# Down projection of a transformer block's SwiGLU in seven block products, weight sums kept in DRAM

## Chip, cores and metric

The kernel runs on one core of one Trainium2 chip. The metric is the device time of one execution in microseconds, median of several runs.

## What is computed

One encoder block for 512 tokens of width 1024: an RMS norm, one combined projection, two kinds of attention, gates, an output projection, and then the channel mixer (width 2816), which is the part that changes:

```python
        h = rms_norm(x, norm_ffn[l])
        x = x + (jax.nn.silu(h @ w_gate_ffn[l]) * (h @ w_up_ffn[l])) @ w_down_ffn[l]

    return rms_norm(x, norm_final)
```

## The kernel before

All data are float32. Each operand of a large matmul is split into a high part in float32r (a cast on ACT, line 68) and the rest (a subtraction on DVE, line 75), and each product is three matmuls, high by high, high by low, low by high (`mm3`, lines 87 to 90). Weights come in units of 128 x 1024 by `load_unit` (lines 77 to 85): SP issues the load into one of 3 raw buffers, ACT casts it to `whi`, DVE subtracts to `wlo`; `whi` and `wlo` have 5 buffers each.

The channel mixer starts at line 585. The 2816 columns are 22 tiles f of 128. `ffn_in(f)` (line 596) computes gate and up of one f for all 512 tokens with 48 matmuls of 128x512 into the PSUM tiles `pg` and `pu` (two buffers each), then ACT takes the sigmoid, DVE multiplies twice into `sg`, and the result is split into `ah` and `al`, which hold the activations of all 22 tiles. The first two f run in two halves of 256 tokens. The down projection multiplies 128-token slices of `ah` and `al` with units of w_down; a unit has two f and one half (512) of the 1024 output columns. For the first column half (units 0 to 10) `down0(u)` runs among the gate/up blocks, 24 matmuls for each pair of f, into four PSUM accumulators `pd`, one for each row tile of 128 tokens. For the second column half (units 11 to 21) the same runs behind the last gate/up block (lines 664 to 674); there the accumulator of the last row tile is in two halves of 256 columns, and the last two units are taken row tile by row tile, so that each row tile can be finished while the next is computed. `residual` (line 649) adds an accumulator to `x1` on DVE, ACT sums the squares, DVE multiplies by the final norm's gain; then POOL takes the power -0.5 (line 683), ACT and DVE scale one half each, and ACT and SP issue the stores of `out`.

The program is written in the order of the work, and a scheduler of the framework places the instructions of each engine by its own estimates; each engine then runs its instructions in that order.

Of the kernel before, what the change touches and what calls it, by code (L numbers as in the profile page):

```python
# [26 lines left out]
NF = FF // P  # L27
UNIT = 1024
# [6 lines left out]
def kernel(  # L35
# [220 lines left out]
    def group_a():  # L256
# [199 lines left out]
    pr = ps_hd.tile([P, S], F32, tag="hd", name="pr")  # L456
# [31 lines left out]
    for qd in range(4):  # L488
# [29 lines left out]
    x1 = x1p.tile([P, NT, DM], F32, name="x1")  # L518
# [42 lines left out]
    accs = [ps_o.tile([P, S], F32, tag="po", name=f"po0_{tt}") for tt in range(NT)]  # L561
# [10 lines left out]
    for tt in range(NT):  # L572
        acc = ps_o.tile([P, S], F32, tag="po", name=f"po1_{tt}")
# [8 lines left out]
    mixer.close()  # L582


    ffn = ExitStack()
    ap_ = pool(ffn, "ap")
    ah = ap_.tile([P, NF, S], F32R, name="ah")
    al = ap_.tile([P, NF, S], F32R, name="al")
# [22 lines left out]
    def down(acc, u, wu, tt, c0=0, c1=S):  # L611
        hi, lo = wu
        t = slice(tt * P, (tt + 1) * P)
        for j in range(2):
            f = 2 * u + j
            w = slice(j * S + c0, j * S + c1)
            mm3(acc, ah[:, f, t], al[:, f, t], hi[:, w], lo[:, w], f == 0, f == NF - 1)
# [15 lines left out]
    for f in range(1, NF):  # L633
        if f > 1:
            ffn_in(f, 0, S, *gu(f))
        if f == 1:
            acc0 = [ps_d.tile([P, S], F32, tag="pd", name=f"pd0_{tt}") for tt in range(NT)]
        if f >= 3 and f % 2 == 1:
            u = (f - 3) // 2
            down0(u)  # L640
    down0(10)
# [14 lines left out]
    v.memset(s3, 0.0)  # L656
    for tt in range(NT):
        residual(tt, 0, S, acc0[tt], 0)
    acc1 = [[(ps_d.tile([P, S], F32, tag="pd", name=f"pd1_{tt}"), 0, S)] for tt in range(NT - 1)]
    H = S // 2  # L660
    acc1.append([(ps_d.tile([P, S], F32, tag="pd", name="pd1_3")[:, :H], 0, H),
                 (ps_g.tile([P, S], F32, tag="pg", name="pd1_4")[:, :H], H, S)])
    NLAST = 2
    for u in range(11 - NLAST):
        wu = load_unit(w_down[11 + u], f"d1_{u}")
        for tt in range(NT):
            for acc, c0, c1 in acc1[tt]:
                down(acc, u, wu, tt, c0, c1)
    last = [load_unit(w_down[11 + u], f"d1_{u}") for u in range(11 - NLAST, 11)]
    for tt in range(NT):  # L670
        for i, (acc, c0, c1) in enumerate(acc1[tt]):
            for u in range(NLAST):
                down(acc, 11 - NLAST + u, last[u], tt, c0, c1)
            residual(tt, S + c0, S + c1, acc, 1 + i)
        n = 1 + len(acc1[tt])
# [93 lines left out]
```

## Time and profile before

| | |
|---|---|
| runs | 767.14, 767.30, 767.84 us; median 767.3 |
| profiled execution | 766.71 us |
| span of its instructions | 764.7 us, 9837 instructions |
| mean granted TensorE clock | 0.995 |
| PE, PE weight load | 745.6 us (97%), 638.5 us (83%) |
| DVE, ACT, POOL | 412.5 us, 337.2 us, 102.7 us |
| DMA | 69.52 MB, 90 GB/s over the span |

The profiled execution lasts 2.0 us longer than the span from its first to its last instruction. Matmuls are pipelined: each lasts longer than the distance to the next, so the busy time of PE says that it had no gap, and the distance of starts says what a matmul costs. A wait is put down to what came last before it.

### The profile page before, as it was taken

The numbers are of one execution on the slowest core, as the hardware profiler recorded it, in microseconds if no ns is written. First come the engines' busy times: TensorE is split into PE (matmuls) and PEld (weight loads), VectorE is DVE, ScalarE is ACT, GpSimd is POOL, SyncE is SP. The second block draws the span as 40 slices with busy tenths as digits, with TensorE's granted clock in tenths as the row PEclk, the third lists the DMA queues.
The fourth block names the chain that finished last, engine by engine and source line by source line (L and its number), as shares of the span: only waits on it lengthen the run. The fifth ranks groups of instructions, "written<-read, shape, count | busy, mean of one in ns | idle before, by whom it ended". The sixth has DMA issues, their size and how long they took to land.

```text
span 764.7 us, 9837 instructions
## 1 busy us (share of the span) xinstructions
PE 745.6 (97%) x3786; PEld 638.5 (83%) x3786; DVE 412.5 (54%) x668; ACT 337.2 (44%) x606; POOL 102.7 (13%) x126
## 2 busy tenths in 40 slices
PE   5999999999999999999999999999999999999996
PEld 4889887799988888888889888888888888888885
DVE  5778698669795564494375433332423333335114
ACT  6457698777667665232153222222222322233203
POOL 3656342223221010100000000000000000000001
PEclk9999999999999999999999999999999999999998
DMA  8122021002141212344223332323232333232202
GB/s 331 64 84 83 29 68 58 21 22 85 29 136 60 78 56 83 137 138 138 82 83 111 111 109 84 110 86 108 86 107 91 102 94 100 90 103 84 82 1 111
DMA packets 21071, 69.52 MB, mean 91 GB/s; under 512 B 2592, under 2 KB 2848, under 8 KB 21024
## 3 DMA queue, kind: packets, MB, share of 16 engines
q1 hardware_dynamic: 18432, 63.45, 25.1%
q10 hardware_dynamic: 2592, 5.45, 2.0%
q8 instruction: 30, 0.49, 0.3%
q14 instruction: 17, 0.14, 0.1%
HBM read 66.79 MB, written 2.10 MB: 90 GB/s over the span
## 4 chain that ended last, share of the span: by engine, by line
PE 94%; DVE 2%; DMA 2%; ACT 1%; issue 1%; POOL 0%; POOLq 0%; ACTq 0%; SPq 0%; DVEq 0%
PE pg L89 5%; PE pu L89 5%; PE pu L90 5%; PE pg L90 5%; PE pg L88 5%; PE pu L88 5%; PE pd L89 5%; PE pd L88 5%; PE pd L90 5%; PE gt L89 4%; PE gt L88 4%; PE gt L90 4%; PE acc_b L89 3%; PE acc_b L88 3%; PE acc_b L90 3%; PE pp L88 2%
## 5 line engine op out<-in xcount | busy, mean ns | idle before, releaser
L89 PE MATMUL pd<-wlo_d,ah 128*128 128x512 f32 (+1 forms) x198 | 72.5, 366 | 0.0
L88 PE MATMUL pd<-whi_d,ah 128*128 128x512 f32 (+1 forms) x198 | 72.4, 366 | 0.0
L90 PE MATMUL pd<-whi_d,al 128*128 128x512 f32 (+1 forms) x198 | 72.0, 365 | 0.0
L88 PE MATMUL pg<-hh,whi_fg 128*128 128x512 f32 (+1 forms) x192 | 71.4, 372 | 0.0
L90 PE MATMUL pu<-hh,wlo_fu 128*128 128x512 f32 (+1 forms) x192 | 71.4, 372 | 0.0
L89 PE MATMUL pg<-hl,whi_fg 128*128 128x512 f32 (+1 forms) x192 | 71.3, 371 | 0.0
L88 PE MATMUL pu<-hh,whi_fu 128*128 128x512 f32 (+1 forms) x192 | 71.3, 371 | 0.0
L89 PE MATMUL pu<-hl,whi_fu 128*128 128x512 f32 (+1 forms) x192 | 71.3, 371 | 0.0
L90 PE MATMUL pg<-hh,wlo_fg 128*128 128x512 f32 (+1 forms) x192 | 71.3, 371 | 0.0
L75 DVE TENSOR_TENSOR wlo_d<-raw_d,whi_d 128x1024 fp32r<-128x1024 f32 x22 | 26.9, 1225 | 72.4 <-ACT whi_d L68 72.4
L75 DVE TENSOR_TENSOR wlo_fg<-raw_fg,whi_fg 128x1024 fp32r<-128x1024 f32 x22 | 27.0, 1225 | 70.0 <-ACT whi_fg L68 69.9
L68 ACT CAST whi_d<-raw_d 128x1024 fp32r<-128x1024 f32 x22 | 23.2, 1053 | 85.4 <-issue 42.3
L68 ACT CAST whi_fg<-raw_fg 128x1024 fp32r<-128x1024 f32 x22 | 23.2, 1053 | 78.8 <-PE pg L89 41.2
L68 ACT CAST whi_fu<-raw_fu 128x1024 fp32r<-128x1024 f32 x22 | 23.2, 1053 | 72.7 <-PE pu L89 69.1
L88 PE MATMUL gt<-xgh,whi_g 128*128 128x512 f32 x128 | 50.6, 395 | 0.0
L90 PE MATMUL gt<-xgh,wlo_g 128*128 128x512 f32 x128 | 50.5, 395 | 0.0
L89 PE MATMUL gt<-xgl,whi_g 128*128 128x512 f32 x128 | 50.5, 394 | 0.0
L683 POOL TENSOR_TENSOR r<-mf,mhalf 128x1 f32<-128x1 f32 x4 | 2.3, 586 | 356.9 <-DVE mf L681 356.9
L607 DVE TENSOR_TENSOR sg<-pu,sg 128x512 f32<-128x512 f32 (+1 forms) x24 | 15.4, 646 | 54.8 <-PE pu L90 54.8
L89 PE MATMUL acc_b<-wlo_b,xgh 128*128 128x384 f32 x128 | 43.6, 341 | 0.0
L90 PE MATMUL acc_b<-whi_b,xgl 128*128 128x384 f32 x128 | 43.4, 339 | 0.0
L88 PE MATMUL acc_b<-whi_b,xgh 128*128 128x384 f32 x128 | 43.3, 339 | 0.0
(278 smaller groups left out, 1832.9 us busy)
## 6 DMA issues: line engine op xcount, KB each, us to landing
raw_fg<-in_w_gu_dram SPq DMA_DIRECT2D x22, 512.0 KB, 3.3
raw_fu<-in_w_gu_dram SPq DMA_DIRECT2D x22, 512.0 KB, 3.3
raw_d<-in_w_down_dram SPq DMA_DIRECT2D x22, 512.0 KB, 3.3
raw_g<-in_w_in_dram SPq DMA_DIRECT2D x16, 512.0 KB, 3.3
raw_b<-in_w_in_dram SPq DMA_DIRECT2D x16, 384.0 KB, 3.6
raw_p<-in_w_proj_dram SPq DMA_DIRECT2D x8, 512.0 KB, 3.3
raw_o<-in_w_out_dram SPq DMA_DIRECT2D x8, 512.0 KB, 3.3
raq<-in_w_in_dram SPq DMA_DIRECT2D x4, 512.0 KB, 7.3
```

Source lines behind the costliest of these rows:

```text
L68: a.copy(dst, src)
L75: v.tensor_tensor(out=dst, in0=src, in1=hi.bitcast(F32), op=ALU.subtract)
L88: pe.matmul(acc, lhsT=lh, rhs=rh, start=start, stop=False)
L89: pe.matmul(acc, lhsT=lh, rhs=rl, start=False, stop=False)
L90: pe.matmul(acc, lhsT=ll, rhs=rh, start=False, stop=stop)
L607: v.tensor_tensor(out=t_, in0=pu, in1=t_, op=ALU.mult)
L683: g.tensor_tensor(out=r3, in0=ms, in1=mhalf[:, 0:1], op=ALU.pow)
```

## The change

The down projection is one product of a 512 x 2816 matrix (tokens by f) with a 2816 x 1024 matrix. It is now taken as two by two blocks: tokens 0 to 255 and 256 to 511, even and odd tiles f, output columns 0 to 511 and 512 to 1023. Eight block products become seven, by Strassen's scheme in Winograd's form. Each block product has 11 tiles of 128 in the contraction and two row tiles.

The products of the first block row, `p1` (even f) and `p2` (odd f), run among the gate/up blocks in `down0(u)`, 12 matmuls for each pair of f, with splits `eh`, `el` of the first 256 tokens only. The five others are kept for later: `sums_a(u)` makes four sums of activation blocks on DVE (128x256 each) and a copy on ACT, kept in float32 in SBUF; `sums_w(u)` loads the other column half of w_down too (`raw_r`, in a buffer of its own), makes four differences of weight blocks on DVE (128x512) and stores them from POOL to DRAM (`tdram`). Behind the last gate/up block come the products "1", "2", "4", "3" and "22" in steps p of two contraction tiles: SP loads 128x1024 of the stored sums (for "4" two halves of w_down itself), ACT and DVE split them, and ACT and DVE split the sum of activations (`sh`, `sl`, 3 buffers each). Accumulators go on from one product to the next without being cleared (`fresh` false): the final values of a block are read by DVE adds into `x1` at the right moments (`add`). The last product has its last row tile in two halves of columns, its last two steps are taken row tile by row tile. Output rows 0 to 255 are finished and stored before it.

```diff
-        split_hi(ah[:, f, t0:t1], t_)
-        split_lo(al[:, f, t0:t1], t_, ah[:, f, t0:t1])
...
+        if t0 == 0:
+            h = sp_.tile([P, M], F32R, tag="eh", bufs=4, name=f"eh{f}")
+            l = sp_.tile([P, M], F32R, tag="el", bufs=4, name=f"el{f}")
+            split_hi(h, acts[f][:, :M])
+            split_lo(l, acts[f][:, :M], h)
+            parts_a[f] = (h, l)
+
+    def sums_a(u):
+        e, o = acts[2 * u], acts[2 * u + 1]
+        s = {n: t[:, u, :] for n, t in sums.items()}
+        v.tensor_tensor(out=s["1"], in0=e[:, M:], in1=o[:, M:], op=ALU.add)
+        v.tensor_tensor(out=s["2"], in0=s["1"], in1=e[:, :M], op=ALU.subtract)
+        v.tensor_tensor(out=s["3"], in0=e[:, :M], in1=e[:, M:], op=ALU.subtract)
+        v.tensor_tensor(out=s["4"], in0=o[:, :M], in1=s["2"], op=ALU.subtract)
+        a.copy(s["22"], o[:, M:])
...
+        def put(i, in0, in1):
+            t = tp_.tile([P, S], F32, tag=f"t{i}", bufs=1 if i else 2, name=f"tw{i}_{u}")
+            v.tensor_tensor(out=t, in0=in0, in1=in1, op=ALU.subtract)
+            g.dma_start(tdram[i][p][:, k * S:(k + 1) * S], t)
+            return t
+
+        t1 = put(0, b12, b11)
+        t2 = put(1, b22, t1)
+        put(2, b22, b12)
+        put(3, t2, b21)
...
     def down0(u):
-        wu = load_unit(w_down[u], f"d0_{u}")
-        for tt in range(NT):
-            down(acc0[tt], u, wu, tt)
+        left = load_raw(w_down[u], f"l{u}")
+        hi, lo = split_unit(left, f"d{u}")
+        right = load_raw(w_down[NU + u], f"r{u}", True)
+        sums_w(u, left, right)
+        for j, accs, loose in ((0, p1, True), (1, p2, False)):
+            h, l = parts_a[2 * u + j]
+            w = slice(j * S, (j + 1) * S)
+            for b in range(2):
+                t = slice(b * P, (b + 1) * P)
+                mm3(accs[b], h[:, t], l[:, t], hi[:, w], lo[:, w], u == 0, u == NU - 1, loose)
...
+    def product(nm, i, accs, fresh, loose, ps):
+        for p in ps:
+            wt, st = weights(i, p), stat(nm, p)
+            for b in range(2):
+                times(accs[b], st, wt, p, b, fresh, loose)
...
+    pr_ = grab("pg", "pr")
+    product("1", 0, pr_, True, True, range(1))
+    down0(NU - 1)
...
+    for b in range(2):
+        add(b, 0, S, p1[b])
+    product("1", 0, pr_, True, True, range(1, NP))
+    for b in range(2):
+        add(b, 0, S, p2[b])
+        finish(b, 0, S, 0)
+    product("2", 1, p1, False, True, range(NP))
+    for b in range(2):
+        add(2 + b, S, DM, pr_[b])
+
+    product("4", None, pr_, False, True, range(NP))
+    for b in range(2):
+        add(b, S, DM, p1[b])
+    product("3", 2, p1, False, True, range(NP))
+    for b in range(2):
+        add(b, S, DM, pr_[b])
+        finish(b, S, DM, 1)
+        write(b, 2)
```

The last product follows (`weights(3, p)`, `stat("22", p)`, into `outs`, three accumulators): after its first four steps come `add(2 + b, 0, S, p1[b])`, `add(2 + b, S, DM, p1[b])` and `finish` for both row tiles, at its end `add` with a subtraction, `finish` and `write`.

Three places of the changed order are of weight.

SP's queue among the gate/up blocks. `raw_fg`, `raw_fu` are gate and up units, `raw_d` units of w_down. Before:

```order
L80 DMA raw_d_2_4971<-in_w_down_dram 128x1024
L80 DMA raw_fg_5001<-in_w_gu_dram 128x1024
L80 DMA raw_fu_5007<-in_w_gu_dram 128x1024
L80 DMA raw_fg_5069<-in_w_gu_dram 128x1024
L80 DMA raw_fu_5075<-in_w_gu_dram 128x1024
```

Now, `raw_l` being the left column half of pair 2 and `raw_r` the right one of pair 3:

```order
L637 DMA raw_l_5038<-in_w_down_dram 128x1024
L637 DMA raw_r_5221<-in_w_down_dram 128x1024
L80 DMA raw_fg_5070<-in_w_gu_dram 128x1024
L80 DMA raw_fu_5076<-in_w_gu_dram 128x1024
L80 DMA raw_fg_5140<-in_w_gu_dram 128x1024
L80 DMA raw_fu_5146<-in_w_gu_dram 128x1024
```

Each pair has one more load, and the right half of the next pair stands ahead of four gate/up loads.

DVE at the passage from product "3" to the last one. `wlo_t` and `sl` are weight and stationary splits of the steps, `x` gets the adds, `xg` the norm products:

```order
L75 TENSOR_TENSOR wlo_t_2_6965<-raw_t_2_6962,whi_t_2_6964 128x1024
L75 TENSOR_TENSOR sl_1_6941<-s_4242,sh_1_6940 128x512
L740 TENSOR_TENSOR x_3873<-x_3873,p_0_4535 128x512 x2
L740 TENSOR_TENSOR x_3873<-x_3873,p_1_4536 128x512 x2
L75 TENSOR_TENSOR wlo_t_3_6993<-raw_t_3_6990,whi_t_3_6992 128x1024
L75 TENSOR_TENSOR sl_2_6969<-s_4242,sh_2_6968 128x512
L746 TENSOR_TENSOR xg<-x_3873,gfin 128x512
L75 TENSOR_TENSOR wlo_t_4_7031<-raw_t_4_7028,whi_t_4_7030 128x1024
```

Before, the adds of the first column half stood among weight splits in the same way, once, without stationary splits:

```order
L75 TENSOR_TENSOR wlo_d_3_6332<-raw_d_3_6329,whi_d_3_6331 128x1024
L651 TENSOR_TENSOR x_3873<-pd_0_4499,x_3873 128x512
L651 TENSOR_TENSOR x_3873<-pd_1_4500,x_3873 128x512
L654 TENSOR_TENSOR xg<-x_3873,gfin 128x512 x2
L678 TENSOR_SCALAR bf_6574<-s_6193 128x1
L651 TENSOR_TENSOR x_3873<-pd_2_4501,x_3873 128x512
```

The adds now stand at every passage from product to product, between the splits of the next product's second and third step.

PE at the start of one step of product "2" (step 1), accumulators `p_0` and `p_1`:

```order
L88 MATMUL p_0_4535<-whi_t_1_6512,sh_1_6516 128x512
L89 MATMUL p_0_4535<-wlo_t_1_6513,sh_1_6516 128x512
L88 MATMUL p_1_4536<-whi_t_1_6512,sh_1_6516 128x512
L89 MATMUL p_1_4536<-wlo_t_1_6513,sh_1_6516 128x512
L90 MATMUL p_0_4535<-whi_t_1_6512,sl_1_6517 128x512
L88 MATMUL p_0_4535<-whi_t_1_6512,sh_1_6516 128x512
```

Before, the three matmuls of one tile followed each other:

```order
L88 MATMUL pd_1_6217<-whi_d_6_6439,ah 128x512
L89 MATMUL pd_1_6217<-wlo_d_6_6440,ah 128x512
L90 MATMUL pd_1_6217<-whi_d_6_6439,al 128x512
L88 MATMUL pd_2_6218<-whi_d_6_6439,ah 128x512
L89 MATMUL pd_2_6218<-wlo_d_6_6440,ah 128x512
```

In the step the matmuls with the low stationary half `sl` come behind the first two of both accumulators. All of PE's program has 3526 rows before and 3427 now.

## Rows read from the trace of the kernel before

**Rows 1.** The page, busy time by engine.
```profile
PE 745.6 (97%) x3786; PEld 638.5 (83%) x3786; DVE 412.5 (54%) x668; ACT 337.2 (44%) x606; POOL 102.7 (13%) x126
```

**Rows 2.** Table of stretches: us, busy PE, PEld, DVE, ACT, POOL, PEclk, DMA share, GB/s.
```profile
...
0.00:20.00 20.00, 9.85 (x64) 9.44 (x64) 11.39 (x15) 12.48 (x17) 8.31 (x9) 1.00 0.89 335
...
395.00:400.00 5.00, 5.00 (x43) 4.92 (x43) 4.51 (x6) 2.87 (x5) 0.00 (x0) 1.00 0.79 243
400.00:700.00 300.00, 300.00 (x1410) 252.01 (x1409) 116.94 (x142) 84.71 (x115) 0.55 (x1) 1.00 0.31 100
700.00:758.00 58.00, 58.00 (x313) 50.31 (x312) 14.35 (x22) 10.34 (x17) 1.33 (x3) 1.00 0.16 55
```

**Rows 3.** Waits of the SP queue from 395 us on: us in total, times, longest.
```profile
...
SPq L80 <- DVE wlo_d L75: 87.2, 17, 5.3
```

**Rows 4.** Groups by shape, PE: busy us, mean ns.
```profile
...
L88 PE MATMUL pd<-whi_d,ah 128*128 128x512 f32 x154 | 60.0, 390 | 0.0
...
L88 PE MATMUL pd<-whi_d,ah 128*128 128x256 f32 x44 | 12.4, 282 | 0.0
```

**Rows 5.** Timeline of PE, one unit of the second column half: start us, us.
```profile
...
710.20 0.39 PE L89 MATMUL pd<-wlo_d,ah 128*128 128x512 f32 x1
...
712.46 0.39 PE L90 MATMUL pd<-whi_d,al 128*128 128x512 f32 x1
712.69 0.28 PE L88 MATMUL pd<-whi_d,ah 128*128 128x256 f32 x1
...
714.00 0.28 PE L90 MATMUL pd<-whi_d,al 128*128 128x256 f32 x1
```

**Rows 6.** Groups by shape, DVE, from 400 us on.
```profile
...
L75 DVE TENSOR_TENSOR wlo_d<-raw_d,whi_d 128x1024 fp32r<-128x1024 f32 x22 | 26.9, 1225 | 72.4 <-ACT whi_d L68 72.4
...
L607 DVE TENSOR_TENSOR sg<-pu,sg 128x512 f32<-128x512 f32 x20 | 13.8, 692 | 54.0 <-PE pu L90 54.0
...
L75 DVE TENSOR_TENSOR al<-sg,ah 128x512 fp32r<-128x512 f32 x20 | 13.7, 684 | 0.0
L651 DVE TENSOR_TENSOR x<-pd,x 128x512 f32<-128x512 f32 x7 | 4.7, 687 | 17.1 <-PE pd L90 17.1
...
L687 DVE TENSOR_SCALAR xg<-xg,r 128x512 f32<-128x512 f32 x4 | 1.9, 485 | 2.0 <-POOL r L683 2.0
...
L75 DVE TENSOR_TENSOR al<-sg,ah 128x256 fp32r<-128x256 f32 x4 | 1.6, 418 | 0.1
```

**Rows 7.** Groups by shape, ACT, from 400 us on.
```profile
...
L68 ACT CAST whi_d<-raw_d 128x1024 fp32r<-128x1024 f32 x22 | 23.2, 1053 | 85.4 <-issue 42.3 <-PE pd L90 29.7 <-PE pu L89 9.2
...
L68 ACT CAST ah<-sg 128x512 fp32r<-128x512 f32 x20 | 12.3, 614 | 0.0
L605 ACT ACTIVATE sg<-pg 128x512 f32<-128x512 f32 x20 | 11.8, 589 | 0.0
...
L68 ACT CAST ah<-sg 128x256 fp32r<-128x256 f32 x4 | 1.5, 404 | 1.3 <-DVE sg L607 1.3
```

**Rows 8.** DMA issues: times issued, KB each, median us to landing.
```profile
...
raw_d<-in_w_down_dram SPq DMA_DIRECT2D x22, 512.0 KB, 3.3
...
raq<-in_w_in_dram SPq DMA_DIRECT2D x4, 512.0 KB, 7.3
...
out_dram<-xg ACTq DMA_DIRECT2D x4, 256.0 KB, 2.4
```

**Rows 9.** Tile raw_fg: landing of its 22 loads.
```profile
DMA to landing us min/median/max: 3.1/3.3/4.9
```

**Rows 10.** Timeline of the end: the third row tile, then the last matmul.
```profile
...
755.32 0.39 PE L90 MATMUL pd<-whi_d,al 128*128 128x512 f32 x1
...
755.75 0.69 DVE L651 TENSOR_TENSOR x<-pd,x 128x512 f32<-128x512 f32 x1
...
758.30 0.28 PE L90 MATMUL pd<-whi_d,al 128*128 128x256 f32 x1
...
758.62 0.42 DVE L651 TENSOR_TENSOR x<-pd,x 128x256 f32<-128x256 f32 x1 [0.55 <-PE pd L90]
...
761.32 0.34 ACTq L686 DMA_DIRECT2D out_dram<-xg  x1
```

More of the change, by code (lines that the diff above doesn't have):

```diff
@@ L582 @@
     mixer.close()
+    NU = NF // 2
+    NP = (NU + 1) // 2
+    M = S // 2
     ffn = ExitStack()
     ap_ = pool(ffn, "ap")
-    ah = ap_.tile([P, NF, S], F32R, name="ah")
-    al = ap_.tile([P, NF, S], F32R, name="al")
+    sums = {n: ap_.tile([P, NU, M], F32, name=f"s{n}") for n in ("1", "2", "3", "4", "22")}
+    sp_ = pool(ffn, "sp", bufs=3)
+    tp_ = pool(ffn, "tp", bufs=3)
+    dr = pool(ffn, "dr", space=bass.MemoryType.DRAM)
+    tdram = [[dr.tile([P, 2 * S], F32, name=f"td{i}_{p}") for p in range(NP)] for i in range(4)]
     fin = ExitStack()
@@ L592 @@
     ps_g = pool(fin, "ps_g", bufs=2, space=PSUM)
-    gfin = ft.tile([P, DM], F32, bufs=1, name="gfin")
-    nc.scalar.dma_start(gfin, norm_final.partition_broadcast(P))
+    raws, acts, parts_a = {}, {}, {}
     def ffn_in(f, t0, t1, ug, uu):
@@ L607, in ffn_in @@
         v.tensor_tensor(out=t_, in0=pu, in1=t_, op=ALU.mult)
-        split_hi(ah[:, f, t0:t1], t_)
-        split_lo(al[:, f, t0:t1], t_, ah[:, f, t0:t1])
[L611 to L617, printed above, removed]
+        if t0 == 0:
+            h = sp_.tile([P, M], F32R, tag="eh", bufs=4, name=f"eh{f}")
[3 more added lines that the diff above has]
+            parts_a[f] = (h, l)
@@ new lines, in sums_a, with load_raw @@
+    def sums_a(u):
[6 more added lines that the diff above has]
+        a.copy(s["22"], o[:, M:])
+    def load_raw(src, nm, own=False):
+        raw = tp_.tile([P, UNIT], F32, tag="rr", bufs=1, name=f"raw_{nm}") if own else wp.tile([P, UNIT], F32, tag="raw", bufs=3, name=f"raw_{nm}")
+        nc.sync.dma_start(raw, src)
+        return raw
@@ new lines, in split_unit, with sums_w @@
+    def split_unit(raw, nm, n=UNIT):
+        hi = wp.tile([P, UNIT], F32R, tag="whi", name=f"whi_{nm}")[:, :n]
+        lo = wp.tile([P, UNIT], F32R, tag="wlo", name=f"wlo_{nm}")[:, :n]
+        split_hi(hi, raw[:, :n])
+        split_lo(lo, raw[:, :n], hi)
+        return hi, lo
+    def sums_w(u, left, right):
+        b11, b21, b12, b22 = left[:, :S], left[:, S:], right[:, :S], right[:, S:]
+        p, k = divmod(u, 2)
+        def put(i, in0, in1):
[7 more added lines that the diff above has]
+        put(3, t2, b21)
@@ new lines, in weights, with stat @@
+    def weights(i, p):
+        n = min(2, NU - 2 * p)
+        raw = wp.tile([P, UNIT], F32, tag="raw", bufs=3, name=f"raw_t{i}_{p}")
+        if i is None:
+            for k in range(n):
+                nc.sync.dma_start(raw[:, k * S:(k + 1) * S], w_down[NU + 2 * p + k][:, S:])
+        else:
+            nc.sync.dma_start(raw[:, :n * S], tdram[i][p][:, :n * S])
+        return split_unit(raw, f"t{i}_{p}", n * S)
+    def stat(nm, p):
+        n = min(2, NU - 2 * p) * M
+        src = sums[nm][:, 2 * p:min(2 * p + 2, NU), :].rearrange("p k t -> p (k t)")
+        h = sp_.tile([P, S], F32R, tag="sh", name=f"sh{nm}_{p}")[:, :n]
+        l = sp_.tile([P, S], F32R, tag="sl", name=f"sl{nm}_{p}")[:, :n]
+        split_hi(h, src)
+        split_lo(l, src, h)
+        return h, l
@@ new lines, in times @@
+    def times(acc, st, wt, p, b, fresh, loose, c0=0, c1=S):
+        for k in range(min(2, NU - 2 * p)):
+            t = slice(k * M + b * P, k * M + (b + 1) * P)
+            w = slice(k * S + c0, k * S + c1)
+            mm3(acc, st[0][:, t], st[1][:, t], wt[0][:, w], wt[1][:, w], fresh and p + k == 0, 2 * p + k == NU - 1, loose)
+    def product(nm, i, accs, fresh, loose, ps):
[3 more added lines that the diff above has]
+                times(accs[b], st, wt, p, b, fresh, loose)
@@ L632, with grab @@
             ffn_in(f, t0, t0 + 256, *gu01[f])
[L633 to L641, printed above, removed]
+    sums_a(0)
+    p1 = [ps_d.tile([P, S], F32, tag="pd", name=f"p1_{b}") for b in range(2)]
+    p2 = [ps_d.tile([P, S], F32, tag="pd", name=f"p2_{b}") for b in range(2)]
+    for f in range(2, NF):
+        ffn_in(f, 0, S, *gu(f))
+        if f % 2 == 1:
+            sums_a(f // 2)
+            down0(f // 2 - 1)
+    def grab(tag, nm):
+        return [ps_g.tile([P, S], F32, tag=tag, name=f"{nm}_{b}") for b in range(2)]
+    pr_ = grab("pg", "pr")
+    product("1", 0, pr_, True, True, range(1))
+    down0(NU - 1)
     s3 = const.tile([P, 3, NT], F32, name="s3")
@@ L647, with add, finish, write @@
     xg = xgp_.tile([P, NT, DM], F32, name="xg")
-    def residual(tt, lo_, hi_, acc, i):
+    gfin = xgp_.tile([P, DM], F32, name="gfin")
+    nc.scalar.dma_start(gfin, norm_final.partition_broadcast(P))
+    def add(tt, lo_, hi_, acc, op=ALU.add):
         xs = x1[:, tt, lo_:hi_]
-        v.tensor_tensor(out=xs, in0=acc, in1=xs, op=ALU.add)
-        jk = ft.tile([P, S], F32, tag="jk", name=f"jk{tt}_{i}")[:, :hi_ - lo_]
+        v.tensor_tensor(out=xs, in0=xs, in1=acc, op=op)
+    def finish(tt, lo_, hi_, i):
+        xs = x1[:, tt, lo_:hi_]
+        jk = xgp_.tile([P, S], F32, tag="jk", bufs=2, name=f"jk{tt}_{i}")[:, :hi_ - lo_]
         a.activation(jk, xs, AF.Square, accum_out=s3[:, i, tt:tt + 1])
         v.tensor_tensor(out=xg[:, tt, lo_:hi_], in0=xs, in1=gfin[:, lo_:hi_], op=ALU.mult)
[L656 to L675, printed above, removed]
+    def write(tt, n):
         ms = small.tile([P, 1], F32, tag="mf", name=f"mf_{tt}")
@@ L688 @@
         nc.sync.dma_start(out[rows, S:], xg[:, tt, S:])
+    v.memset(s3, 0.0)
+    for b in range(2):
[15 more added lines that the diff above has]
+        write(b, 2)
+    H = S // 2
+    p4 = grab("pu", "p4")
+    half = ps_d.tile([P, S], F32, tag="pd", name="p4_h")[:, :H]
+    outs = [[(p4[0], 0, S)], [(p4[1][:, :H], 0, H), (half, H, S)]]
+    NLAST = 2
+    for p in range(NP - NLAST):
+        wt, st = weights(3, p), stat("22", p)
+        for b in range(2):
+            for acc, c0, c1 in outs[b]:
+                times(acc, st, wt, p, b, True, False, c0, c1)
+    for b in range(2):
+        add(2 + b, 0, S, p1[b])
+        add(2 + b, S, DM, p1[b])
+        finish(2 + b, S, DM, 0)
+    last = [(weights(3, p), stat("22", p)) for p in range(NP - NLAST, NP)]
+    for b in range(2):
+        for i, (acc, c0, c1) in enumerate(outs[b]):
+            for k, (wt, st) in enumerate(last):
+                times(acc, st, wt, NP - NLAST + k, b, True, False, c0, c1)
+            add(2 + b, c0, c1, acc, ALU.subtract)
+            finish(2 + b, c0, c1, 1 + i)
+        write(2 + b, 1 + len(outs[b]))
     fin.close()
```

13 lines of the change are left out of this document (7 added, 6 removed).

## The prediction

> **What bounds the kernel now.** I read the page's busy line first, then a table of stretches, then the shapes of the down projection's matmuls, then single rows of the matmul stream. TensorE (PE) is busy for 745.6 of 764.7 us, VectorE (DVE) for 412.5, ScalarE (ACT) for 337.2 [rows 1]. From the first gate matmul to the last down matmul PE is busy in every microsecond at the full clock: 5.00 of 5, 300.00 of 300, 58.00 of 58 [rows 2]. DVE is busy 39% of the long stretch (116.94 of 300) and 25% of the next. Nobody makes PE wait there, so the stretch is worth its matmuls. What ends a load's wait for its buffer is a DVE split that itself waited for PE: "SPq L80 <- DVE wlo_d" is 87.2 us of waiting that costs nothing [rows 3].
>
> A busy PE row is no price: the 128x512 matmuls overlap, and 390 ns each [rows 4] is their latency. The price is the distance of their starts. Ten full ones run from 710.20 to 712.46: 0.226 to 0.227 us each; eleven half ones (128x256) from 712.69 to 714.00: 0.119 us [rows 5].
>
> **The change, matmuls.** Before: three lines of 154 full and 44 half matmuls, 462 + 132 [rows 4]. After: seven products, eleven contraction tiles each, two output row tiles, three matmuls: 7 x 11 x 2 x 3 = 462, of which the 33 of the last row tile are cut in two: 429 full + 66 half. PE's program is 99 rows shorter, which is this difference. Removed: 33 full x 0.2267 = 7.5 us, 66 half x 0.119 = 7.9 us, together **15.4 us**, all on the path.
>
> By the Trainium skill, TensorE: Matmul & The Clock Gate, Back-to-back issue gap, an isolated warm matmul of N columns costs N/2.4 + 2.5 ns, by which the same removal would be 33 x 0.216 + 66 x 0.109 = 14.3 us; it is an estimate from that page. The rows are longer by 5 to 9%, and they are this kernel's own stream, so the sum takes the rows.
>
> **What is added, gate/up stage.** A pair of f takes PE 96 + 12 = 108 matmuls = 24.5 us (120, 27.2 us, before). DVE per pair, by its rows [rows 6]: five weight splits of 1.225, four gate products of 0.69, two low halves of 0.42, four activation sums of 128x256 at 0.42, four weight differences of 128x512 at 0.69, some 0.3 of the first S1 splits: 14.5 us, 59%. ACT: five casts of 1.053, two sigmoids and the small casts at 0.4 to 0.6 [rows 7]: some 8.5 us. Both fit. The activation splits are halved here (only the first 256 tokens), which is counted.
>
> Two queues are moved past. On SP each pair has one more load, raw_r of the next pair, right behind raw_l; with a single buffer it waits until DVE has made the differences of this pair, and four gate/up loads stand behind it. DVE makes them after the first f of the pair is done, because raw_l itself waits for a split there: then raw_r is issued about 18 us into the pair, the first gate load behind it lands by about 23 us (landing 3.3, at most 4.9 [rows 8, 9]), and PE wants its split at about 49, two pairs after the start of this one. I cost this at nothing; the cover is the five split tiles of the ring (about two dozen us), and only when it is gone does each late microsecond count. On POOL, idle in this stage (0.55 us in 300 [rows 2]), stand 44 stores of 256 KB. The trace has no store issued by POOL; the same 256 KB from ACT lands in 2.4 us [rows 8]. Its reader is the next use of the same tile a pair later, some 20 us, or a product some 20 us later or more, so between 0 and 20 us of landing time it costs nothing. I take 0. The first of them sits on POOL ahead of the four small operations of the FFN norm, for which PE would wait; it depends on one load that SP issues between two w_out loads, a whole output projection earlier, so I leave it at 0 too.
>
> **What is added, products.** Behind the last gate/up block PE has five products without cover by gate/up. A full step of two tiles is 12 matmuls, 2.72 us, and needs a 512 KB load, a weight split (ACT 1.053, DVE 1.225) and a stationary split (ACT 0.614, DVE 0.684): ACT 1.67, DVE 1.91 of 2.72 us. A product is 66 matmuls, 15.0 us; its DVE splits are 5 x 1.225 + 0.69 + 5 x 0.684 + 0.42 = 10.7 us. The accumulator adds (0.69 each, [rows 6]), norm products (0.69) and scalings (0.485) come on top. Heaviest are the stretches under products "1" and the last one (four adds, two norm products: 14.8 us) and under "3" (two adds, two norm products, two scalings: 14.4 us). That is 96 to 99% of 15.0, against 25% now: DVE becomes the second bound, and just holds. What is late next: in program order the adds of a finished product stand behind the third weight split of the next one and ahead of its third stationary split. At the end of product "3" the queue is four adds 2.8, a weight split 1.2, a stationary split 0.7, together 4.7 us from the product's end; PE has two steps ready, 5.4 us. A margin of 0.7 us; elsewhere it is 2 to 3. I take no stall, and keep 0 to 2 us here for the range. The adds also free the accumulators: each pair of accumulators has most of a product before it is used again, so nothing waits for that.
>
> The loads: one buffer of three is taken for the landing L plus cast and split, L + 2.3 us, so a step cannot be shorter than (L + 2.3)/3. With the median 3.3 that is 1.9 us, with the worst of the gate loads, 4.9 [rows 9], it is 2.4, both under 2.72. The rate asked is 512 KB per 2.72 us, 193 GB/s; 243 GB/s were moved at the start of the gate/up stage and 335 at the start of the kernel [rows 2]. Cost 0.
>
> **The tail.** Now the third row tile's last matmul starts at 755.32, DVE takes its accumulator at 755.75, and from there DVE is nearly without a gap to the end: when the very last matmul starts (758.30), DVE waits 0.5 us for it (758.62) [rows 10]. After the change six half matmuls fewer, 0.7 us, lie between those two points, in a stretch that DVE sets. So of the 15.4 us some 0.2 to 0.7 come back; I take 0.5.
>
> **Sum.** Profiled execution: 766.71 (span 764.7 and 2.0 around it) - 15.4 + 0.5 = 751.8. The median of the runs, 767.3, is 0.6 above that execution, so the forecast is **752.4 us**.
>
> **Rivals.**
> 1. *Feeding binds in the products* (still faster, less). For it: DVE's 96 to 99% in three of five stretches, a stationary ring of only three tiles, and a PE order in which the matmuls with the low stationary half are put behind the others of their step. Against it: the margins above, in measured durations. If every full step of the five products (25) is stretched by 0.1 to 0.25 us and the stall at the end of product "3" is 2 us, 4 to 8 us are lost: 756 to 760.5.
> 2. *Slower: the weight sums come back from DRAM too late.* Place: the three raw buffers in the five products. Price: 25 steps x ((L + 2.3)/3 - 2.72). Loss starts at L = 5.9 us; the gain of 14.9 is eaten when a step reaches 3.32 us, L = 7.7; at L = 9, 3.77 us a step, it costs 26 us: 778. For it: these loads read what was stored before, which no row shows, and the four loads raq at the kernel's start took 7.3 in the median [rows 8]. Against it: those came at 335 GB/s [rows 2] with several in flight, and here 193 is asked.
> 3. *The change doesn't do what it says*, the matmuls are not fewer on PE: the count of rows excludes it, beyond what is in the other cases.
>
> **How the numbers follow.** Forecast 0.78, rival 1 0.16, rival 2 with L beyond 7.7 0.04, something without effect on time 0.02. The likeliest case alone is 751.5 to 754.4 (tail 0.2 to 0.7, DVE 0 to 2 us, the spread of the runs). The range adds the lower part of rival 1, and below a microsecond for matmul starts that are closer than the ten I read: 750.8 to 759. A measurement of this kernel can tell about 0.2%, 1.5 us: faster 0.94, same 0.01, slower 0.05.
>
> **What would show it.** In the table of stretches PE busy in every microsecond from the gate/up stage to the last product at clock 1.00, with the down matmuls among gate/up shorter by 11 x 12 x 0.2267 = 29.9 us and those behind longer by 14.5 (75.2 for five products against 60.7 for eleven units); DVE over 80% in the last 75 us; loads of the sums landing under 5 us; the tail from last matmul to end 0.5 us longer. Rival 1 would show as PE idle ended by "DVE sl" or "ACT sh" in the waits; rival 2 as ACT casts of raw_t that wait for a DMA, and PE behind them. The prediction is wrong if PE idles over 2 us in the products, or if the starts of full matmuls lie further apart than 0.227 us.

## The result

The changed kernel takes **753.1 us** (median of four runs, 752.75 to 754.17), the kernel before beside it 767.2: a ratio of 0.982, 95% interval 0.9803 to 0.9837. It is faster by 14.1 us. The forecast was 752.4, in a range of 750.8 to 759.0. The profiled execution takes 752.75 us, its span is 751.0.

The page's busy line of the changed kernel, to be held against [rows 1]:

```profile
PE 730.7 (97%) x3687; PEld 625.1 (83%) x3687; DVE 491.5 (65%) x811; ACT 367.6 (49%) x664; POOL 128.9 (17%) x170
```

PE has 99 rows fewer and is busy 14.9 us less; DVE has 79 us more, ACT 30, POOL 26. Where that lies is in the table of stretches (columns as in [rows 2]):

```profile
396.00:640.00 244.00, 244.00 (x1177) 206.34 (x1176) 136.94 (x200) 75.61 (x109) 21.83 (x41) 1.00 0.51 172
...
665.00:680.00 15.00, 15.00 (x68) 12.43 (x67) 12.53 (x20) 7.97 (x14) 0.00 (x0) 1.00 0.55 177
680.00:695.00 15.00, 15.00 (x68) 12.43 (x67) 11.45 (x14) 8.78 (x14) 0.00 (x0) 1.00 0.58 192
695.00:710.00 15.00, 15.00 (x67) 12.41 (x67) 11.49 (x15) 8.73 (x13) 0.00 (x0) 1.00 0.59 194
710.00:725.00 15.00, 15.00 (x68) 12.41 (x67) 13.54 (x21) 11.08 (x19) 2.77 (x2) 1.00 0.60 206
725.00:740.00 15.00, 15.00 (x90) 13.36 (x89) 11.35 (x18) 7.28 (x13) 0.00 (x0) 1.00 0.32 111
665.00:743.00 78.00, 78.00 (x374) 65.69 (x373) 61.09 (x88) 43.85 (x68) 2.77 (x2) 1.00 0.51 169
```

Up to the first product (396 to 640) and through all five (665 to 743) PE is busy in every microsecond at the full clock, as before the change [rows 2]. In none of these stretches is DVE busy more than 13.54 of 15 us. They begin up to 3.5 us ahead of the products. Cut at the products' own first matmuls (665.81, 683.49, 698.45, 713.41 and 728.37 us) DVE is busy for 14.37 of 17.68 us in "1", which has the 12 matmuls of the last pair in it, then for 11.45, 11.45 and 13.49 of 14.96 in "2", "4" and "3", and for 10.22 of 15.33 in the last one. PE's waits name none between its first gate matmul (396.23) and its last down matmul.

That last one starts at 743.70, 347.47 us behind the first gate matmul; before it was 758.30 - 395.29 = 363.01. So PE's stream is **15.54 us** shorter. Around it two things go the other way. The first gate matmul starts 0.94 us later, and PE's very first one 0.84 us later (6.76 us, 5.92 before), ahead of anything that the change touches; and from the last matmul to the end of the span it is 7.30 us, not 6.40. -15.54 + 0.94 + 0.90 = -13.7, the difference of the spans.

The price of a matmul has stayed. In PE's timeline ten full ones of product "1" take from 675.79 to 678.05, 0.226 us each, as in [rows 5]:

```profile
675.79 0.39 PE L90 MATMUL pr<-whi_t,sl 128*128 128x512 f32 x1
...
678.05 0.39 PE L88 MATMUL pr<-whi_t,sh 128*128 128x512 f32 x1
```

The DMA issues (times issued, KB each, median us to landing):

```profile
td<-tw POOLq DMA_DIRECT2D x44, 256.0 KB, 4.5
raw_fg<-in_w_gu_dram SPq DMA_DIRECT2D x22, 512.0 KB, 4.4
...
raw_t<-td SPq DMA_DIRECT2D x20, 512.0 KB, 3.9
```

The stores from POOL land in 4.5 us, the sums read back in 3.9, and the gate loads in 4.4 where it was 3.3 [rows 9].

DVE's groups by shape between 665 and 743 us (busy us, mean ns, what it waited for):

```profile
L75 DVE TENSOR_TENSOR wlo_t<-raw_t,whi_t 128x1024 fp32r<-128x1024 f32 x18 | 22.0, 1221 | 2.5 <-ACT whi_t L68 2.4
L75 DVE TENSOR_TENSOR sl<-s,sh 128x512 fp32r<-128x512 f32 x22 | 15.1, 687 | 6.9 <-ACT sh L68 5.3 <-PE pr L89 1.0 <-PE p L89 0.5
L740 DVE TENSOR_TENSOR x<-x,p 128x512 f32<-128x512 f32 x11 | 7.0, 681 | 4.5 <-PE p L90 4.5
...
```

All fifteen groups of this view add up to 65.8 us of rows, while the table of stretches has DVE busy for 61.09: rows that follow each other overlap, by 0.05 us in the mean of all 88. Where two stand back to back it is more: below, a row of 0.69 us starts at 742.95 and the next one at 743.56, 0.61 later.

The end, in the timeline:

```profile
742.23 0.69 DVE L740 TENSOR_TENSOR x<-x,p 128x512 f32<-128x512 f32 x1 [4.49 <-PE p L90]
...
742.95 0.69 DVE L746 TENSOR_TENSOR xg<-x,gfin 128x512 f32<-128x512 f32 x1
...
743.56 0.41 DVE L740 TENSOR_TENSOR x<-x,p 128x256 f32<-128x256 f32 x1
...
743.70 0.28 PE L90 MATMUL p_h<-whi_t,sl 128*128 128x256 f32 x1
...
744.01 0.42 DVE L740 TENSOR_TENSOR x<-x,p_h 128x256 f32<-128x256 f32 x1
...
744.35 0.75 DVE L746 TENSOR_TENSOR xg<-x,gfin 128x256 f32<-128x256 f32 x2
...
745.09 0.48 DVE L760 TENSOR_SCALAR xg<-xg,r 128x512 f32<-128x512 f32 x1
745.49 0.15 DVE L754 SCALAR_TENSOR_TENSOR mf<-s,bf 128x1 f32<-128x1 f32 x1
...
747.05 0.34 ACTq L759 DMA_DIRECT2D out_dram<-xg  x1
```

### The profile page after: what moved, and what is told of

Read it like the earlier page. It is cut to its first block, busy times and chain, and to the rows that moved or that the text cites. A ratio compares the mean times of both kernels' runs of the same rounds, so it can differ in the third digit from the quotient of the medians.

```text
span 751.0 us, 10105 instructions
## 1 busy us (share of the span) xinstructions
PE 730.7 (97%) x3687; PEld 625.1 (83%) x3687; DVE 491.5 (65%) x811; ACT 367.6 (49%) x664; POOL 128.9 (17%) x170
## 4 chain that ended last, share of the span: by engine, by line
PE 94%; DVE 2%; DMA 2%; ACT 1%; issue 1%; POOLq 0%; POOL 0%; ACTq 0%; DVEq 0%
PE pu L90 5%; PE pg L90 5%; PE pg L89 5%; PE pu L89 5%; PE pg L88 5%; PE pu L88 5%; PE gt L89 4%; PE gt L88 4%; PE gt L90 4%; PE p L89 3%; PE p L88 3%; PE p L90 3%; PE acc_b L89 3%; PE acc_b L88 3%; PE acc_b L90 3%; PE pp L88 2%
## 5 line engine op out<-in xcount | busy, mean ns | idle before, releaser
L654 POOL DMA_DIRECT2D td<-tw x44 | 24.0, 546 | 269.8 <-DVE tw L653 220.4
L75 DVE TENSOR_TENSOR wlo_fg<-raw_fg,whi_fg 128x1024 fp32r<-128x1024 f32 x22 | 26.9, 1222 | 24.5 <-ACT whi_fg L68 24.3
L89 PEld LDWEIGHTS pu<-hl,whi_fu 128*128 128x128 f32 x192 | 36.2, 188 | 6.3
L89 PEld LDWEIGHTS pg<-hl,whi_fg 128*128 128x128 f32 x192 | 36.2, 188 | 6.3
L88 PEld LDWEIGHTS pg<-hh,whi_fg 128*128 128x128 f32 x192 | 36.2, 188 | 6.2
L88 PEld LDWEIGHTS pu<-hh,whi_fu 128*128 128x128 f32 x192 | 36.2, 188 | 6.2
L90 PEld LDWEIGHTS pg<-hh,wlo_fg 128*128 128x128 f32 x192 | 36.2, 188 | 6.2
L90 PEld LDWEIGHTS pu<-hh,wlo_fu 128*128 128x128 f32 x192 | 36.2, 188 | 6.2
```

Of the source, the lines that this page charges most:

```text
L88: pe.matmul(acc, lhsT=lh, rhs=rh, start=start, stop=False, skip_group_check=loose)
L89: pe.matmul(acc, lhsT=lh, rhs=rl, start=False, stop=False, skip_group_check=loose)
L90: pe.matmul(acc, lhsT=ll, rhs=rh, start=False, stop=stop, skip_group_check=loose)
L654: g.dma_start(tdram[i][p][:, k * S:(k + 1) * S], t)
```

## The experiments

All but the first of these kernels are the changed kernel with one edit. They ran in three groups, each on one chip beside the kernel before (768.6 to 768.9 us there): the first four; then the two with extra DVE work, the ring of stationary tiles and the first run on the tail; last the weight loads' ring and the other two runs on the tail. Since the start of a kernel varies by more than most of these edits are worth, each is also read from its trace by one number, the **stream**: first gate matmul to last down matmul, 363.01 us before and 347.47 in the changed kernel.

**The matmuls alone.** The kernel before, with as many matmuls left out as the change removes:

```diff
+    SKIP = {1, 3, 4, 5, 7, 9, 10, 11, 13, 15, 17}
-    def down(acc, u, wu, tt, c0=0, c1=S):
+    def down(acc, u, wu, tt, c0=0, c1=S, skip=()):
             f = 2 * u + j
+            if f in skip:
+                continue
-                down(acc, u, wu, tt, c0, c1)
+                down(acc, u, wu, tt, c0, c1, SKIP if tt >= 2 else ())
```

> The kernel before with the matmuls of 11 of the 22 f left out for the last two row tiles of the second half: 33 full (128x512) and 66 half (128x256) matmuls of the down projection fewer, as many as the change removes, and nothing added. That part of the computation is missing. All f left out lie ahead of the last two units, so the tail is as before. Theory (the matmuls are worth the distance of their starts, all on the path): 33 x 0.2267 + 66 x 0.119 = 15.4 us off, 767.2 to 751.8, the stretch from the first gate matmul to the last down matmul 15.4 us shorter, PE without a wait in it. By the rule in the Trainium skill, TensorE: Matmul & The Clock Gate, Back-to-back issue gap, it would be 14.3 us, an estimate. Rival (what bounds the second half is feeding as soon as a unit has fewer matmuls): under 12 us off, with PE waits on wlo_d or whi_d. The rest, this time less the 753.1 of the change, is what all the added work costs: 1.3 us if the theory holds.

Measured: 753.42 us against 768.55, ratio 0.980 (0.9785 to 0.9812). Its first gate and last down matmul in PE's timeline:

```profile
397.68 0.28 PE L88 MATMUL pg<-hh,whi_fg 128*128 128x256 f32 x1
...
745.25 0.28 PE L90 MATMUL pd<-whi_d,al 128*128 128x256 f32 x1
```

The stream is 347.57 us, **15.44 us shorter**, within 0.1 us of what the distances of the starts give, and its tail (last matmul to the end of the span) is 6.45 us, as before. PE's waits name none in the stream, so the rival falls. This kernel, which carries none of the change's added work, and the changed kernel have the same stream within 0.1 us. So everything that the change adds costs nothing there.

**The stores and the way through DRAM.** Three edits:

```diff
-            g.dma_start(tdram[i][p][:, k * S:(k + 1) * S], t)
+            nc.scalar.dma_start(tdram[i][p][:, k * S:(k + 1) * S], t)
```

> The changed kernel with the 44 stores of the weight sums issued by ACT, not by POOL. Theory A (the 0.9 us by which the changed kernel's first matmul starts later, 6.8 against 5.9 us, come with POOL's use of the software queue, and the stores cost nothing at their own place): first matmul at 5.9 again, 752.2 us. Theory B (that 0.9 is chance or has to do with something else of the change): first matmul at 6.8 as in the changed kernel, 753.1 us. Rival C (ACT waits in its order for a DVE difference ahead of each store, and the casts behind it come late): PE waits among gate and up, over 754 us.

```diff
-            nc.sync.dma_start(raw[:, :n * S], tdram[i][p][:, :n * S])
+            nc.sync.dma_start(raw[:, :n * S], w_down[NU + 2 * p][:, :n * S])
```

> The changed kernel with the four products '1', '2', '3' and '22' loading a block of the down weights as it is instead of the sum of weight blocks from DRAM; differences and stores are still made, but nobody reads them back, so these four products are of other numbers. Theory (reading back what was stored costs nothing, the loads of 512 KB land in 3.9 us where 5.9 would be needed for a loss): 753.1 us, within 0.5. Rival (the sums come back late, by the store or by the read): over 1 us faster than the changed kernel, and the loads of raw_t land over 1 us sooner than its 3.9.

The same edit, and the stores gone:

```diff
-            g.dma_start(tdram[i][p][:, k * S:(k + 1) * S], t)
```

> As the run that loads the down weights as they are, and the 44 stores left out as well (the differences are still made by DVE): the sums of weight blocks are missing from the computation. Theory A (POOL's software queue delays the kernel's start): first matmul at 5.9, 752.2 us. Theory B (it doesn't): first matmul at 6.8, 753.1 us. Rival (44 stores of 256 KB take the loads' time in the gate/up stage): over 1.5 us faster than the changed kernel, the gain lying between the first gate matmul and the first product.

Measured: 753.11, 753.82 and 753.73 us, ratios 0.980 each (0.9784 to 0.9810, 0.9790 to 0.9817, 0.9788 to 0.9815); streams of 347.46, 347.47 and 347.46. The DMA rows of the three, in this order:

```profile
td<-tw ACTq DMA_DIRECT2D x44, 256.0 KB, 4.4
```

```profile
raw_t<-in_w_down_dram SPq DMA_DIRECT2D x20, 512.0 KB, 4.1
```

```profile
raw_fg<-in_w_gu_dram SPq DMA_DIRECT2D x22, 512.0 KB, 3.9
```

Loads of plain weights land no sooner (4.1) than those of stored sums (3.9), and leaving the stores out brings the stream nothing. The gate loads land in 3.9 us there; with the stores it is 4.4 in the changed kernel, but 4.0 with ACT's, and more than half of what they are over the 3.3 of [rows 9] is there without any store. Rival C of the first run and the rivals of the other two fall. Theory A of the start falls too, though the first matmul of the first run alone would have borne it out: the first matmul is at 5.95 without POOL's stores, but at 5.86 with them (the second kernel). For the whole time, no run differs from another by what its interval could tell.

**What DVE has to spare.** One more difference in each step of a product, of full and of half width:

```diff
         split_lo(l, src, h)
+        split_lo(tp_.tile([P, S], F32R, tag="xx", bufs=2, name=f"xx{nm}_{p}")[:, :n], src, h)
```

> The changed kernel with one more DVE difference in every step of the five products (128x512, into a scratch tile that nobody reads): 5 of 512 and 1 of 256 columns a product. Read from the first gate matmul to the last down matmul, 347.5 us in the changed kernel. Theory A (DVE rows cost the distance of their starts, 0.61 and 0.33 us, and DVE is 11.5 to 13.5 of 15 us busy in a product as the changed kernel's table of stretches shows): 3.4 us more a product, 14.9 to 16.9 of 15.0, so 2 to 4 us longer in all, with DVE at 95% and more. Theory B (rows cost their full duration, as the prediction counted, 14.4 to 14.8 us in three of five products): 3.9 us more, 18.3 of 15 in three products and 16 in two, so some 12 us longer. Rival C (DVE is not near a bound): under 1 us.

> The same with an extra DVE difference of half the width (128x256, 128x128 in the short step). Theory A: 1.9 us more a product, 13.4 to 15.4 of 15.0: 0 to 1 us longer from the first gate matmul to the last down matmul. Theory B: 2.4 us more a product, 16.9 of 15 in three of them: some 6 us longer. Rival C: 0.

Measured: 756.41 us (ratio 0.984, 0.9829 to 0.9858) and 754.14 (0.981, 0.9794 to 0.9827). Streams: 348.41 and 347.44. The products in the table of stretches, first with the full, then with the half difference:

```profile
665.00:743.00 78.00, 77.48 (x366) 64.76 (x365) 73.89 (x113) 44.29 (x69) 5.12 (x2) 1.00 0.52 171
```

```profile
665.00:743.00 78.00, 78.00 (x371) 65.57 (x370) 68.34 (x114) 44.95 (x71) 3.44 (x2) 1.00 0.52 172
```

With DVE at 73.89 of 78 us (95%, 61.09 in the changed kernel) PE loses 0.94 us, with 68.34 (88%) nothing. PE's waits in the stream name one in the first run and none in the second:

```profile
PE p L90 <- DVE sl L75: 0.5, 1, 0.5
```

Theory B, the prediction's count, is far off (12 us and 6). Theory A has the extra work about right (12.8 us for 25 more rows, every sixth of half width) but the loss of the first run too high, 2 to 4 us. It filled each product by itself; that one product carries another's surplus would explain the difference, which no run shows. By its figures rival C, under 1 us and 0, holds in both runs, but the wait on a DVE split shows that at 95% DVE is at the edge of a bound. Most of the rest of the 2.8 us by which the first is slower than the changed kernel on another chip (753.64) lies in the tail, 8.8 us for 7.3: here the scheduler ends PE's program with the last matmuls of both row tiles together, and DVE then has three accumulators to take. The half one has that too (8.4).

**The ring of stationary tiles.** `bufs=2` at the tiles `sh` and `sl`, for three:

> The changed kernel with two stationary tiles of each kind in the products' ring where it has three. Theory (the prediction's cover: at a product's end DVE has 4.7 us of adds and splits ahead of the next stationary split, and PE two prepared steps, 5.4 us; with one prepared step, 2.7 us, it runs dry): up to 2 us lost at each of the ends of products that have four accumulator operations behind them, 2 to 6 us in all, as PE waits on sl or sh. Rival (the scheduler's order spreads the adds, and DVE has more room than was counted): under 1 us.

Measured: 755.95 us (ratio 0.984, 0.9824 to 0.9853), stream 348.47, **1.00 us longer**. PE's waits in the stream name one:

```profile
PE p L90 <- DVE sl L75: 0.4, 1, 0.4
```

It is the wait that was foreseen, on the low half of a stationary split, but one where several were expected, and the loss is half of the theory's lowest figure and at the edge of the rival's (under 1 us): the theory's place holds, its size doesn't. The tail is 9.1 us, by the same other order of the last matmuls.

**The weight loads' ring.** `tag="raw", bufs=2` for 3:

> The changed kernel with two raw buffers for weight loads where it has three (in the whole kernel; the scheduler orders parts of it otherwise). Theory (the prediction's rule for the loads: a step of a product can't be shorter than (landing + cast + split)/buffers): with the measured landing of 3.9 us, (3.9 + 2.3)/2 = 3.1 us a step against 2.72, 0.38 us lost in each of 25 full steps, so the products take 87 instead of 78 us, some 9.5 us more, with PE waits on the casts and splits of the weights and these waiting for their loads; among gate and up, five loads of 3.1 us in 24.5 us, nothing lost. Rival (the five split tiles ahead of PE and the order of the loads cover it): under 2 us more in the products.

Measured: 762.64 us (ratio 0.992, 0.9907 to 0.9934), 9.0 more than the changed kernel beside it (753.64). The stream is 353.75, **6.28 us longer**; 3.6 us more lie ahead of it (the start varies, and earlier stages use the same ring), and the tail is 8.57. In the table of stretches:

```profile
665.00:680.00 15.00, 15.00 (x68) 12.43 (x67) 11.54 (x20) 8.00 (x14) 0.00 (x0) 1.00 0.54 169
680.00:695.00 15.00, 15.00 (x68) 12.43 (x67) 11.08 (x14) 7.86 (x11) 0.00 (x0) 1.00 0.50 167
695.00:710.00 15.00, 15.00 (x68) 12.43 (x67) 9.75 (x12) 7.64 (x10) 0.00 (x0) 1.00 0.49 161
710.00:725.00 15.00, 12.83 (x50) 9.79 (x49) 9.73 (x15) 8.25 (x15) 0.00 (x0) 0.89 0.51 158
...
720.00:721.00 1.00, 0.90 (x3) 0.67 (x3) 1.00 (x3) 0.83 (x2) 0.00 (x0) 0.50 0.52 106
...
722.00:723.00 1.00, 1.00 (x4) 0.71 (x4) 1.00 (x1) 0.19 (x1) 0.00 (x0) 0.50 0.18 70
```

From 665 to 710 us PE loses nothing, so it is not the steady 0.38 us a step that the rule gives; the loads landed in 3.2 us here, and with that the rule says 2.75 for 2.72. The loss begins at one place: a load issued at 711.48 takes 5.7 us to land, the longest of all the loads of raw_t in this run, ACT's cast of its weight waits 2.81 us for it, the stationary cast stands behind it on ACT, and PE waits for that. ACT in the timeline, then PE's waits in the stream, then what ACT waited for ahead of all its casts of raw_t (us, times):

```profile
717.28 1.04 ACT L68 CAST whi_t<-raw_t 128x1024 fp32r<-128x1024 f32 x1 [2.81 <-DMA raw_t<-td]
718.23 1.14 ACT L68 CAST sh<-s 128x512 fp32r<-128x512 f32 x2
```

```profile
PE p L88 <- ACT sh L68: 2.1, 1, 2.1
PE p L89 <- DVE wlo_t L75: 0.8, 2, 0.5
PE p L88 <- ACT whi_t L68: 0.2, 1, 0.2
```

```profile
  DMA raw_t<-td: 22.4, 16
```

In the changed kernel that last line is 1.7 us, once. The two lower lines of PE's waits are in the last product, on splits and a cast of weights as the theory has it, 1.0 us in all. And after the long wait the clock falls: PE's rows stand at 0.50 of full speed from 720 to 723 us, the lower of its two levels (1.2 for 2.4 GHz), and from 720.24 to 723.36 seven matmuls take 3.12 us, where seven times 0.227 is 1.59:

```profile
718.89 0.50 PE L88 MATMUL p<-whi_t,sh 128*128 128x512 f32 x1 [2.07 <-ACT sh L68]
...
720.24 0.79 PE L90 MATMUL p<-whi_t,sl 128*128 128x512 f32 x1
...
723.36 0.40 PE L90 MATMUL p<-whi_t,sl 128*128 128x512 f32 x1
```

The waits named (3.1 us) and the slow matmuls (1.5) are 4.6 of the 6.28 us; the remaining 1.7 are not put down to anything here.

**The tail.**

```diff
-        a.activation(xg[:, tt, 0:S], xg[:, tt, 0:S], AF.Copy, scale=r3)
-        nc.scalar.dma_start(out[rows, 0:S], xg[:, tt, 0:S])
+        c = {2: 768, 3: 384}.get(tt, S)
+        a.activation(xg[:, tt, 0:c], xg[:, tt, 0:c], AF.Copy, scale=r3)
+        (nc.sync if tt == 2 else nc.scalar).dma_start(out[rows, 0:c], xg[:, tt, 0:c])
...
```

> The changed kernel with another share of the last scalings: the third row tile's is 768 columns on ACT and 256 on DVE (512 and 512 before), its store is issued by SP alone, the last row tile's 384 on ACT and 640 on DVE. Theory (in the changed kernel's tail DVE's scaling of the third row tile, 0.48 us, stands ahead of the sum mf that the last one waits for): mf 0.2 us earlier, ACT's last scaling 0.15 us shorter, the last store issued 3.0 instead of 3.35 us behind the last matmul: 0.3 to 0.4 us off the span, less than the runs' spread. Rival (the last store's landing, 3.4 to 3.95 us, sets the end and varies by more): nothing to be seen, 753 to 754 us.

> The kernel with the other share of the last scalings once more, beside the changed kernel on one chip. Theory (the last store is issued 0.24 us sooner, and its landing gives part of that back): 0 to 0.3 us faster than the changed kernel, not to be told from it by the interval. Rival (the sooner store counts in full, with more): over 0.5 us faster.

> The changed kernel once more, on the chip of its neighbours here. Theory (the 0.9 us later first matmul of its first profile and the differences of up to 2.8 us in the start of the first gate matmul between runs of other kernels lie ahead of the change and come with the chip and the run): a first gate matmul somewhere between 395.3 and 398.1 us, 347.5 us from there to the last down matmul, 7.0 to 7.3 us of tail, 753 to 754 us. Rival (the changed kernel itself starts late): its first matmul at 6.8 again and a first gate matmul at least 0.9 us behind that of the kernel with other last scalings.

Measured: 753.65 us; then, on one chip, 753.03 (ratio 0.980, 0.9786 to 0.9813) against 753.64 for the changed kernel (0.980, 0.9787 to 0.9814). The last store is issued 3.11 us behind the last matmul in both profiles, not 3.35, where 3.0 was worked out; in the timeline of the first:

```profile
744.80 0.28 PE L90 MATMUL p_h<-whi_t,sl 128*128 128x256 f32 x1
...
746.20 0.34 DVE L761 TENSOR_SCALAR xg<-xg,r 128x256 f32<-128x256 f32 x1
746.46 0.15 DVE L754 SCALAR_TENSOR_TENSOR mf<-s,bf 128x1 f32<-128x1 f32 x1
...
747.91 0.35 ACTq L760 DMA_DIRECT2D out_dram<-xg  x1
```

But from there to the end it is 3.99 and 3.92 us, 3.90 in the changed kernel beside the second, and the tails are 7.10 and 7.03 us for 7.25: 0.2 us are left, which these intervals cannot tell from nothing. The first run's 753.65 is what its rival has (753 to 754, nothing to be seen). The medians of the two kernels on one chip lie 0.61 us apart, over the 0.5 of the second run's rival, but their runs spread over 1.5 and 2.0 us, and the trace shows 0.2. So no version is shown to beat the changed kernel.

The changed kernel's second profile answers for the start: first matmul at 5.90, first gate matmul at 395.89, stream 347.46, tail 7.25. The 0.9 us of its first profile was not the change's, and the rival falls. Beside the kernel before on this chip (768.92) the changed kernel is 15.3 us faster, not 14.1. Part of a later start goes with PE's clock between 20 and 40 us; this stretch of the changed kernel's second profile and of the kernel with ACT's stores:

```profile
20.00:40.00 20.00, 19.19 (x101) 17.08 (x102) 15.64 (x30) 9.02 (x16) 11.34 (x14) 0.91 0.12 45
```

```profile
20.00:40.00 20.00, 18.14 (x91) 16.44 (x92) 14.77 (x26) 7.85 (x15) 11.42 (x12) 0.83 0.14 51
```

A mean of 0.91 here, 0.83 there: 0.08 of 20 us is 1.6 of the 2.2 us by which the latter's first gate matmul is later (398.12). It is a part only: the first profile's 0.84 us lay at the first matmul, and at 0.83 in this stretch other runs have a first gate matmul anywhere from 396.7 us on.

## Why the prediction was right

**Matmuls removed, 15.4 us.** Right: 15.54 in the stream, and 15.44 when they alone are removed. The Trainium skill's TensorE: Matmul & The Clock Gate, Back-to-back issue gap, from which 14.3 was estimated, is 1.1 to 1.2 us short here; the distance of starts in the trace was the better price. The split of it was wrong: -29.9 us among gate and up and +14.5 behind were forecast. The last up matmul starts at 662.87, 266.64 us behind the first gate matmul, and 686.40 - 395.29 = 291.11 before: -24.5, and +8.9 behind.

```profile
686.40 0.39 PE L90 MATMUL pu<-hh,wlo_fu 128*128 128x512 f32 x1
```

```profile
662.87 0.39 PE L90 MATMUL pu<-hh,wlo_fu 128*128 128x512 f32 x1
```

All eleven units of the down projection had been counted among gate and up; in both programs two of them stand behind the last up matmul, and nine times 12 x 0.2267 is the 24.5.

**Gate/up stage, DVE 59%, ACT 8.5 us a pair.** 56% (136.94 of 244) and 7.6 us. Right, and both off the path.

**SP's extra load, POOL's 44 stores, the way through DRAM: 0.** Right. The run with plain weights, the run without stores and the run that does nothing but drop matmuls all have the same stream. Loads of the sums landed in 3.9 us; three of 24 took over 5 us, and the point from which they would cost, 5.9, was reached by one (6.0), without a wait of PE. Rival 2 is excluded. Its rule (L + 2.3)/buffers is not borne out: with two buffers and the 3.2 us in which the loads landed there it gives 25 x 0.03, some 0.8 us, where 6.28 were lost, and that 9.5 had been expected from a landing of 3.9 came near by luck. The loss is one load of 5.7 us and what stands behind it in ACT's order, the clock after it, and shorter waits in the last product. Whether 5.9 is the point with three buffers no run tests.

**DVE just holds, 96 to 99% in three of five products, margin 0.7 us.** It held, but this step was wrong in its size: 11.35 to 13.54 of 15 us, 76 to 90%. Product "3" is the heaviest, 13.49 of 14.96 for the 14.4 forecast; the last one, forecast at 14.8, has 10.22 of 15.33, and DVE is through with its last split 6 us before it ends. The prediction priced PE's rows by the distance of their starts and DVE's by their full length; DVE's rows overlap as well, 65.8 us of rows in 61.1 of time. (The Trainium skill, VectorE: DVE Perf Modes, The DRAIN you can't avoid, has an op start before the one ahead is through if nothing holds it; the trace agrees, by 0.05 us a row in the mean.) And three stationary and two weight splits of product "1" were counted in it that the scheduler puts among gate and up: behind 665 us there are 22 + 5 of 30 stationary and 18 + 5 of 25 full weight splits. DVE has between 7.3 and 12.8 us to spare over the five products, by the runs with an extra difference. The 80% that was to show it is 78% in fact. The term stood in the sum as nothing, so the forecast did not depend on how full DVE was. The stall of rival 1 (4 to 8 us, chance 0.16) is not in the changed kernel, and with a stationary tile less it is 1.0 us.

**Tail, +0.5.** +0.90 in the first profile, +0.85 in the second, of which the engines set 0.33 (last store issued 3.35 us behind the last matmul, 3.02 before) and the last stores' way to the end the rest (3.95 and 3.90 us, 3.38 before). The mechanism holds: between the last two accumulators DVE has less time. It takes the third row tile's 1.47 us before the last matmul starts (742.23), before the change 2.55 us (755.75 [rows 10]); the prediction counted 0.7 us less, it is 1.08. The 0.55 us for which DVE had waited are gone by it, and one norm product of half width that lay ahead of the last matmul now lies behind it, at 744.35 as one of two. That is the 0.33; the scaling of 0.48 us ahead of mf stands there in both programs. In the kernel before:

```profile
757.64 0.43 DVE L654 TENSOR_TENSOR xg<-x,gfin 128x256 f32<-128x256 f32 x1
...
759.03 0.48 DVE L687 TENSOR_SCALAR xg<-xg,r 128x512 f32<-128x512 f32 x1
...
759.42 0.42 DVE L654 TENSOR_TENSOR xg<-x,gfin 128x256 f32<-128x256 f32 x1
```

That the stores take longer was not foreseen, and why is open: it is 3.37 to 3.66 in the three runs with other stores or other loads.

**Sum.** 751.8 was forecast for the profiled execution and 752.75 came, 0.94 more: -0.14 by the stream, +0.40 by the tail, +0.94 by a start that varies, -0.26 by the time around the span (1.75 us for 2.01). The median is 0.7 us above the forecast. That the execution without its late start would be the forecast within 0.1 us is luck: the other three terms cancel.

## What to carry to other kernels

Where one engine's rows are back to back, its price is the distance of starts; here that held for VectorE (0.61 us for rows of 0.69) as for TensorE, and a sum of durations overstated how full it was. An engine that feeds another was 78%, even 88%, busy here at no cost with three prepared tiles between them; with two tiles the same load cost 1.0 us. To judge an edit of some microseconds, compare a stretch between two fixed instructions of the traces, not the whole times: here the stretch repeated to 0.03 us over eight profiles in which PE did not wait, while the start moved by 2.2, and by 2.8 with the kernel before.

## What was not expected of the hardware

- After a wait of 2.1 us in a full stream, from about a microsecond after its end, the granted clock was 0.50 for 3 us, and seven full matmuls took 1.5 us longer. It was seen once; waits of 0.4 and 0.5 us in two other runs had no such thing behind them.
- A 256 KB store issued by POOL holds POOL for 0.55 us and lands in 4.5 us; issued by ACT the same 44 stores land in 4.4. The 2.4 us from [rows 8] was that of the stores at the kernel's end; why these take longer no run shows.
- Between executions of kernels that are alike up to there, the first gate matmul started anywhere from 395.3 to 398.1 us.
